# Low parts of 24 weight tiles formed by accumulating transfers, with a new order of block one

## The chip, the core and the metric

The kernel runs on one core of one Trainium2 chip. The metric is the device time of one execution in microseconds. The core has a matrix engine (PE in the profile, with its weight loads as PEld), a vector engine (DVE), a scalar engine (ACT), GpSimd (POOL) and SyncE (SP). SP starts nearly all transfers between the chip's memory (HBM) and the on-chip memory (SBUF). PE writes its results into eight PSUM banks, from where DVE or ACT take them out.

## The reference

Two layers run one after the other on 512 positions of width 1024, batch 1, all in float32. Block one projects the normalised input with one wide matrix and feeds two branches from it: a recurrence over time (eight heads of 64), and an attention that keeps, for each query, the 128 keys with the highest index scores.

```python
xn = rmsnorm(x, norm_g)
p = xn @ w_in                                     # 24 tiles of 128 columns here
p_shift, g_rwkv, q_down, kv_down, k_idx_raw, w_idx, g_attn = jnp.split(p, IN_SPLITS, axis=-1)
...
S = S * w_t + sa * (kk_t * a_t) + v_t * k_t       # rwkv7_scan, over time
y_rwkv = y * jax.nn.silu(gate)
...
_, idx = lax.top_k(score, topk)                   # topk = 128
p = jax.nn.softmax(s, axis=-1)                    # over the chosen keys
y_attn = o * jax.nn.silu(gate)
x = x + jnp.concatenate([y_rwkv, y_attn], axis=-1) @ w_out
```

Block two mixes three branches (a gated 3-tap convolution, a 31-tap convolution with a layer norm, an attention on 256 memory rows), adds a feed-forward net with 2816 channels, and normalises. Its memory rows give keys with `w_k` and values with `w_v`, before anything of block one is known.

## The kernel before

All activations lie transposed: 128 channels on the partitions, 512 positions along a row. A float32 product is made of three fast products (type fp32r). Each operand is split into a high part H, which is its value rounded to fp32r, and a low part L = value − H. PE adds up H·H, H·L and L·H and leaves L·L out. For a weight tile of 128 output columns and 1024 rows (`slab`, L547) SP brings the raw tile into one of four `wr` buffers, ACT writes H into one of three `wh` buffers, and DVE writes L = raw − H into one of three `wl` buffers (`sub`, L353). A tile of `w_in` then takes 24 matmuls with 512 columns: eight rows of blocks, each with two matmuls on H and one on L. `out_half` (L1302) does the same for half a tile of `w_out` (four rows of blocks, 12 matmuls); half 0 takes the recurrence's channels, half 1 those of the attention. The tiles of `w_v` have two rows of blocks with 512 columns, and H and L are the moving operand there (also 12 matmuls). `w_k` is multiplied in plain float32, raw.

`w_in` numbers 0 to 15 are the latents, keys, receptances and values; 16 to 23 are the two gates (`strand_gates`, "gr" and "ga"), which are first needed when a branch ends. The memory strand (`w_k`, `w_v`) is needed in block two alone.

The program is written as a list of operations with groups ("level"), and `Program.order` (L188 on) puts them into one order: it goes on in its own estimate of time, takes of all operations that could start the one that starts first, and among those nearly equal the one with the lowest rank. A rank is the operation's number plus 20000 times its group's entry in the table `LEVEL`. The order is fixed at build time. Each engine executes its own share strictly in that order and waits at semaphores. So a wait of one instruction holds everything behind it on its engine.

In block one the serial work is this: projections, the inverses of 32x32 triangles on DVE, the chain over eight chunks (`strand_chain`), beside it the top-k for three query blocks (16 times MAX8 and MATCH_REPLACE8 on DVE each, `strand_index`), the heads, the attention (`strand_attention`), and last `w_out`. Tiles of weights that nothing waits for yet fill PE in between. GpSimd sets constants, masks the scores, and multiplies the chain's state (`G.tensor_mul`, two for each chunk).

Nearly every operation carries the line of the recorder (L341), `sub` L354, and those that may go to either engine L345 to L360; so tiles name them: `wr`, `wh`, `wl` are weights, `a` activations, `s` small columns, `ps` PSUM, `x` the inverses.

Of the kernel before, what the change touches and what calls it, by code (L numbers as in the profile page):

```python
# [8 lines left out]
F32 = mybir.dt.float32  # L9
F32R = mybir.dt.float32r  # L10
AF = mybir.ActivationFunctionType
ALU = mybir.AluOpType
# [13 lines left out]
NA = 76  # L26
NS = 12
LEVEL = {
# [12 lines left out]
}  # L41
MEMC = 4
BOOST = 0
# [43 lines left out]
class Program:  # L87
# [73 lines left out]
    def cost(self, who, op, outs, ins):  # L161
        n = outs[0].free_size()
        if op == "dma_start":
            return 0.06
        if who == "PE":
            if ins[0].dtype != F32:
                return max(0.0535, n / 2400.0) + 0.0132
            if op == "transpose":
                return 0.107
            m = outs[0].shape[0]  # L170
            return 2 * max(0.107 if m > 64 else 0.056 if m > 32 else 0.029, 2 * n / 2400.0)
        n = max(x.free_size() for x in outs + ins)
        narrow = sum(x.free_size() == 1 for x in ins[1:])
        if who == "V":
            if op in ("max", "match_replace", "tensor_tensor_reduce"):
                return 0.07 + 0.06 * (op == "match_replace") + n / 960.0
            if op in ("tensor_tensor_scan", "transpose"):
                return 0.07 + n / 490.0
            if op == "tensor_mul" and ins[1:] and ins[1].ap[-1][0] > 1 and ins[1].ap[-1][1] > 1:
                return 0.07 + n / 500.0  # L180
            fast = op in ("tensor_copy", "tensor_scalar") and all(x.space != PSUM for x in ins + outs)
            scalar = op == "scalar_tensor_tensor" and len(ins) > 2
            return 0.069 + 0.064 * (scalar or narrow > 0 and op == "tensor_scalar") + n / (1920.0 if fast else 960.0)
        if who == "S":
            return (0.058 if ins[0].space == PSUM else 0.085) + 0.092 * (narrow + len(outs) - 1) + n / 1175.0
        return 0.07 + n / (1250.0 if op == "memset" else 440.0)
# [132 lines left out]
def build(tc, I, O, plan=None):  # L319
# [33 lines left out]
    def sub(out, x, y):  # L353
        prog.add({"V": ("tensor_sub", lambda: nc.vector.tensor_sub(out, x, y))}, [out], [x, y])  # L354
# [34 lines left out]
    def here():  # L389
        return len(prog.nodes) - 1  # L390

    V, S, G, PE, SY = (Queue(e, w) for e, w in ((nc.vector, "V"), (nc.scalar, "S"), (nc.gpsimd, "G"),
                                                 (nc.tensor, "PE"), (nc.sync, "SY")))

    def pooled(pool, shape, dt, tag):
        k = len(pools)
        if plan is None:
            t = pool.tile(list(shape), dt, tag=tag, name=tag, bufs=caps[tag])
        else:
            t = pool.tile(list(shape), dt, tag="%s%d" % (tag, plan[2][k]), name=tag, bufs=1)  # L400
        pools.append(t.tensor.name)
        prog.tag[t.tensor.name] = tag
        return t
# [10 lines left out]
    def A(shape=(128, 512), dt=F32):  # L414
        return pooled(ap_, shape, dt, "a")
# [4 lines left out]
    def SM(n, m=128):  # L420
        return pooled(sp, (m, n), F32, "s")

    def PS():
        return pooled(pp, (128, 512), F32, "ps")
# [106 lines left out]
    def rsqrt(src, n, eps, op=ALU.add, scale=1.0):  # L531

        x, y, t = SM(n), SM(n), SM(n)
        ts(V, x, src, scale, eps, ALU.mult, op)
        ts(V, t.bitcast(I32), x.bitcast(I32), 1, None, ALU.logical_shift_right)
        ts(V, y.bitcast(I32), t.bitcast(I32), -1.0, float(0x5F3759DF), ALU.mult, ALU.add)
        for _ in range(3):
            V.tensor_mul(t, y, y)
            V.scalar_tensor_tensor(t, t, -0.5, x, op0=ALU.mult, op1=ALU.mult)
            V.scalar_tensor_tensor(y, t, 1.5, y, op0=ALU.add, op1=ALU.mult)  # L540
        return y


    def WR(shape):
        return pooled(wp, [128] + list(shape), F32, "wr")

    def slab(name, idx, shape=(8, 128), parts=1):  # L547
        nk = min(shape[0], 8 if name != "w_down" or idx % 3 < 2 else 6)
        raw = WR(shape)
        SY.dma_start(raw[:, 0:nk, :], I[name][idx][:, 0:nk, :])  # L550
        H = pooled(wp, (128,) + shape, F32R, "wh")
        L = pooled(wp, (128,) + shape, F32R, "wl")
        for p in range(parts):
            k = slice(nk * p // parts, nk * (p + 1) // parts)
            S.activation(H[:, k, :], raw[:, k, :], AF.Copy)
            sub(L[:, k, :], raw[:, k, :], H[:, k, :].bitcast(F32))
        return H, L, nk

    def gemm_tile(name, idx, xH, xL, n=512, ps=None, k0=0, ktot=8, parts=1):
        H, L, nk = slab(name, idx, parts=parts)  # L560
        ps = ps or PS()
        for k in range(nk):
            kk = k0 + k
            PE.matmul(ps[:, :n], H[:, k, :], xH[kk], start=kk == 0, stop=False)
            PE.matmul(ps[:, :n], H[:, k, :], xL[kk], start=False, stop=False)
            PE.matmul(ps[:, :n], L[:, k, :], xH[kk], start=False, stop=kk == ktot - 1)
        return ps
# [111 lines left out]
    raw = A()  # L679
    wix = AR_()  # L680
    raw, wix = raw[:, 0:64].rearrange("p (k c) -> p k c", k=8), wix[:, 0:64].rearrange("p (k c) -> p k c", k=8)
# [620 lines left out]
    def out_half(n, half):  # L1302
        raw = WR((4, 128))
        SY.dma_start(raw, I["w_out"][n][:, 4 * half:4 * half + 4, :])
        H = pooled(wp, (128, 4, 128), F32R, "wh")
        L = pooled(wp, (128, 4, 128), F32R, "wl")
        S.activation(H, raw, AF.Copy)
        sub(L, raw, H.bitcast(F32))
        ps = PS()
        for k in range(4):  # L1310
            h, l = yH[4 * half + k], yL[4 * half + k]
            PE.matmul(ps, H[:, k, :], h, start=k == 0, stop=False)
            PE.matmul(ps, H[:, k, :], l, start=False, stop=False)
            PE.matmul(ps, L[:, k, :], h, start=False, stop=k == 3)
        return ps

    for n in range(8):
        xr = A()
        with after(here()):
            SY.dma_start(xr, I["xt"][n])  # L1320
        with level("out%d" % n):
            V.tensor_add(xr, out_half(n, 0), xr)
        X1.append(xr)
    prog.group, prog.offset = "rest", int(LEVEL["rest"] * 20000)
    for n in range(8):
        xr = X1[n]
        V.tensor_add(xr, out_half(n, 1), xr)
        h, l = split_act(xr, Dp("gz", n))
        zH.append(h)
        zL.append(l)  # L1330
        sq = A()
        S.activation(sq, xr, AF.Square)
        ac2 = add_to(ac2, sq, Dp("fgs", n))
        ac1 = add_to(ac1, sq)
# [3 lines left out]
    r1 = rsqrt(sv[:, 0:4], 4, 1e-6)  # L1338
    r2 = SM(4)
    V.tensor_mul(r2, r1, r1)  # L1340
    V.tensor_mul(r2, r2, sv[:, 4:8])
    r2 = rsqrt(r2, 4, 1e-6)
# [81 lines left out]
    for s_ in range(4):  # L1424
        GV = []
        for m in range(2):
            n = 2 * s_ + m
# [99 lines left out]
    for f in range(22):  # L1527
        gu = []
        for m in range(2):
            n = f + 22 * m  # L1530
# [16 lines left out]
    for n in range(7):  # L1547
# [7 lines left out]
        scaled(X3[n], X3[n], P_("fin_g", n))  # L1555

    last = [slab("w_down", 21 + j) for j in range(3)]
    for half in range(2):
        hs = slice(256 * half, 256 * half + 256)
        ps = PS()  # L1560
        for k in range(22):
            H, L = (t[:, k % 8, :] for t in last[k // 8][:2])
# [19 lines left out]
        r2 = rsqrt(st[:, 0:2], 2, 1e-6)  # L1582
# [115 lines left out]
```

## Time and profile before

| | us |
|---|---|
| runs: median (lowest, highest) of 3 | 1377.17 (1376.52, 1382.12) |
| the profiled execution's own time | 1377.95 |
| its span in the trace | 1376.2 |
| PE busy | 1348.1 (98%) |
| DVE busy | 1049.8 (76%) |
| ACT busy | 585.4 (43%) |
| POOL busy | 29.9 (2%) |

The profiled execution took 1377.95 us, 1.75 us more than its span; it stands 0.8 us above the median of the runs. An engine's busy time is the union of its instructions' durations. PE's matmuls are pipelined and their ends are modelled, so a busy PE still can have gaps. Block one ends at about 399.6 us of the span, and from there to 1340 us PE is busy without a gap that the windows show.

### The profile page before, as it was taken

The page shows a single profiled execution, that of the slowest core. Times are in us where ns is not written, and L with a number is a line of the kernel's source. Part 1 is how long each engine was busy: PE and PEld are TensorE (multiplying, and loading weights), DVE is VectorE, ACT ScalarE, POOL GpSimd, SP SyncE. Part 2 cuts the span into 40 slices and gives each one's busy share as a digit, 9 for nine tenths or more (in the row PEclk, how much of TensorE's full clock was granted, in tenths as well). Part 3 has the DMA queues.
Part 4 walks back from the last instruction along what each step waited for, and adds up shares of the span by engine and source line. Part 5 has one row for each costly group of instructions (what it writes and reads, how often), then busy time and mean ns, then how long its engine had stood idle before and what let it go on. Part 6 is the DMA issues. An engine that isn't in the chain of part 4 may idle for free.

```text
span 1376.2 us, 18233 instructions
## 1 busy us (share of the span) xinstructions
PE 1348.1 (98%) x7032; PEld 1121.8 (82%) x7032; DVE 1049.8 (76%) x1902; ACT 585.4 (43%) x945; POOL 29.9 (2%) x68
## 2 busy tenths in 40 slices
PE   7999999999999999999999999999999999999997
PEld 6878877888888888888888878888888888888886
DVE  7699879999699999999993584444577788784333
ACT  6683455668353334322222372223444444442221
POOL 2010002100000000000000000000000000000000
PEclk9999988999999999999999999999999999999999
DMA  6203220031446221233333223233222333322321
GB/s 225 71 20 104 84 72 32 32 100 55 145 146 214 92 77 62 77 101 99 92 98 101 77 92 107 92 98 101 92 92 95 104 92 96 103 88 96 100 70 61
DMA packets 41927, 129.29 MB, mean 94 GB/s; under 512 B 4912, under 2 KB 7088, under 8 KB 41840
## 3 DMA queue, kind: packets, MB, share of 16 engines
q1 hardware_dynamic: 41840, 128.13, 28.8%
q8 instruction: 55, 0.90, 0.3%
q14 instruction: 32, 0.26, 0.1%
HBM read 123.91 MB, written 4.19 MB: 93 GB/s over the span
## 4 chain that ended last, share of the span: by engine, by line
PE 88%; DVE 7%; ACT 3%; issue 1%; POOL 0%; DMA 0%; DVEq 0%; POOLq 0%; ACTq 0%
PE ps L341 88%; DVE a L341 5%; ACT a L341 2%; DVE s L341 1%; DVE wl L354 0%; DVE a L354 0%; ACT a L346 0%; ACT wh L341 0%; DMA wr<-in_w_v 0%; POOL a L341 0%; DVE a L345 0%; POOL mm L341 0%; DVE x L345 0%; ACT a L350 0%; POOL gsel L341 0%
## 5 line engine op out<-in xcount | busy, mean ns | idle before, releaser
L341 PE MATMUL ps<-a,wh 128*128 128x512 f32 (+1 forms) x3276 | 1006.2, 388 | 0.2 <-ACT wh L341 0.2
L341 PEld LDWEIGHTS ps<-a,wh 128*128 128x128 f32 x3276 | 612.1, 188 | 123.5 <-ACT wh L341 0.8
L341 PE MATMUL ps<-a,wl 128*128 128x512 f32 (+1 forms) x1638 | 634.7, 388 | 0.5 <-DVE wl L354 0.5
L341 ACT ACTIVATE wh<-wr 128x1024 fp32r<-128x1024 f32 (+3 forms) x223 | 224.8, 1010 | 490.6 <-PE ps L341 362.3
L341 PEld LDWEIGHTS ps<-a,wl 128*128 128x128 f32 x1638 | 308.2, 188 | 62.8 <-DVE wl L354 1.0
L354 DVE TENSOR_TENSOR wl<-wr,wh 128x1024 fp32r<-128x1024 f32 (+3 forms) x223 | 257.9, 1159 | 78.2 <-ACT wh L341 76.8
L341 DVE SCALAR_TENSOR_TENSOR a<-a,par 128x511 f32<-128x511 f32 (+24 forms) x393 | 273.4, 730 | 5.5 <-ACT a L341 3.1
L341 DVE TENSOR_TENSOR a<-ps,a 128x512 f32<-128x512 f32 (+1 forms) x186 | 117.2, 632 | 113.2 <-PE ps L341 107.2
L341 ACT ACTIVATE a<-a 128x512 f32<-128x512 f32 (+5 forms) x184 | 112.3, 623 | 169.5 <-DVE a L341 151.2
L341 PE MATMUL ps<-a 128*64 128x64 f32 (+10 forms) x1060 | 134.3, 296 | 14.5 <-POOL a L341 7.5
L341 PEld LDWEIGHTS ps<-a 128*64 128x64 f32 (+5 forms) x1040 | 103.5, 170 | 27.3 <-DVE a L341 5.7
L341 DVE SCALAR_TENSOR_TENSOR a<-a 128x512 f32<-128x512 f32 (+3 forms) x112 | 67.7, 611 | 20.3 <-ACT a L341 19.4
L341 DVE TENSOR_TENSOR a<-a 128x512 f32<-128x512 f32 (+5 forms) x134 | 76.0, 585 | 3.0 <-ACT a L341 1.9
L341 ACT ACTIVATE a<-a,par 128x512 f32<-128x512 f32 (+1 forms) x89 | 65.1, 737 | 19.7 <-DVE a L341 18.0
L354 DVE TENSOR_TENSOR a<-a 128x512 fp32r<-128x512 f32 x72 | 48.4, 686 | 18.1 <-ACT a L341 16.1
L341 ACT ACTIVATE a<-ps 128x512 fp32r<-128x512 f32 (+5 forms) x77 | 42.1, 569 | 44.4 <-PE ps L341 33.5
L341 DVE SCALAR_TENSOR_TENSOR a<-a,ps 128x512 f32<-128x512 f32 x24 | 16.5, 686 | 55.5 <-PE ps L341 55.4
L341 ACT ACTIVATE a<-a,dpar 128x512 f32<-128x512 f32 (+2 forms) x57 | 41.6, 733 | 7.6 <-DVE a L341 7.3
L346 ACT ACTIVATE a<-ps 64x256 f32<-64x256 f32 (+5 forms) x74 | 29.5, 409 | 28.3 <-PE ps L341 26.9
L341 PE MATMUL ps<-ident,a 128*128 128x128 f32 x204 | 32.7, 286 | 1.0 <-ACT a L350 0.6
L341 PEld LDWEIGHTS ps<-ident,a 128*128 128x128 f32 x204 | 25.8, 155 | 7.2 <-ACT a L350 1.7
L341 PE MATMUL ps<-a,wr 128*128 128x256 f32 x128 | 29.6, 379 | 0.0
(113 smaller groups left out, 567.7 us busy)
## 6 DMA issues: line engine op xcount, KB each, us to landing
wr<-in_w_in SPq DMA_DIRECT2D x96, 512.0 KB, 3.6
wr<-in_w_up SPq DMA_DIRECT2D x44, 512.0 KB, 3.4
wr<-in_w_down SPq DMA_DIRECT2D x16, 512.0 KB, 3.5
a<-in_xt SPq DMA_DIRECT2D x16, 256.0 KB, 3.5
wr<-in_w_k SPq DMA_DIRECT2D x8, 512.0 KB, 3.6
wr<-in_w_v SPq DMA_DIRECT2D x8, 512.0 KB, 3.6
wr<-in_w_out SPq DMA_DIRECT2D x16, 256.0 KB, 2.7
wr<-in_w_att SPq DMA_DIRECT2D x8, 512.0 KB, 3.5
```

The lines of the kernel that those rows point to most:

```text
L341: prog.add({self.who: (op, lambda: f(*a, **k))}, outs, ins)
L346: "S": ("activation", lambda: nc.scalar.activation(out, src, AF.Copy))}, [out], [src])
L354: prog.add({"V": ("tensor_sub", lambda: nc.vector.tensor_sub(out, x, y))}, [out], [x, y])
```

## The change

The low part can be made in another way. A new function `low` has ACT write −H (rounded like H) into the `wl` buffer, by an activation with scale −1, and has GpSimd start a transfer from HBM that adds the raw weights to what stands there (`accum_op=ALU.add`). DVE's subtraction falls away for the tiles that go this way: `w_in` 16 to 23, all eight tiles of `w_v`, and the 16 half tiles of `w_out`, which makes 32 transfers of 24 tiles' bytes. The table `LEVEL` is replaced as a whole, and the order's own estimate of a transfer's issue on GpSimd goes from 0.06 to 1.0 us. `slab` and `out_half` call `low`; nothing else is changed.

```diff
 LEVEL = {
-    "att0": -0.214, "att1": 1.055, "att2": -0.113, "att3": 1.636, "base": 2.048, "chain": -0.643, "first":
...
+    "att0": 0.372, "att1": -0.274, "att2": 2.672, "att3": 2.806, "base": 0.757, "chain": 2.012, "first":
...
         if op == "dma_start":
-            return 0.06
+            return 1.0 if who == "G" else 0.06
...
+    def low(L, raw, H, src, dma):
+
+        if dma:
+            S.activation(L, raw, AF.Copy, scale=-1.0)
+            G.dma_start(L, src, accum_op=ALU.add)
+        else:
+            sub(L, raw, H.bitcast(F32))
+
...
             S.activation(H[:, k, :], raw[:, k, :], AF.Copy)
-            sub(L[:, k, :], raw[:, k, :], H[:, k, :].bitcast(F32))
+            low(L[:, k, :], raw[:, k, :], H[:, k, :], I[name][idx][:, k, :], name == "w_v" or name == "w_in" and idx > 15)
...
         S.activation(H, raw, AF.Copy)
-        sub(L, raw, H.bitcast(F32))
+        low(L, raw, H, I["w_out"][n][:, 4 * half:4 * half + 4, :], True)
```

What this does to the order is shown at three places. The first is ACT at the second halves of `w_out`, the last work of block one. `wh<-wr` makes H, `a<-a,dpar` and `a<-a` belong to the sum that has come out. Before:

```order
248 L341 ACTIVATE wh<-wr 128x512
249 L341 ACTIVATE a<-a,dpar 128x512
250 L341 ACTIVATE a<-a 128x512
251 L341 ACTIVATE wh<-wr 128x512
252 L341 ACTIVATE a<-a,dpar 128x512
```

Now, with `wl<-wr`, which writes −H:

```order
289 L341 ACTIVATE wh<-wr 128x512
290 L341 ACTIVATE wl<-wr 128x512
291 L341 ACTIVATE a<-a,dpar 128x512
292 L341 ACTIVATE a<-a 128x512
293 L341 ACTIVATE wh<-wr 128x512
294 L341 ACTIVATE wl<-wr 128x512
```

Each half tile now takes two of ACT's instructions in a row, and its low part is ready only when the transfer behind the second has landed.

The second place is GpSimd's queue from the inverse to the start of the chain (`AFFINE_SELECT wr<-wr` and `MEMSET x_403` prepare the inverse, `AFFINE_SELECT a<-a` masks scores, `TENSOR_TENSOR a<-a,pc` is the chain's state). Before:

```order
33 L341 AFFINE_SELECT wr<-wr 128x1024
34 L341 MEMSET a 64x512 x2
35 L341 MEMSET x_403 32x32x32 x2
36 L341 AFFINE_SELECT a<-a 128x128 x2
37 L341 TENSOR_TENSOR a<-a,pc 128x256 x2
```

Now:

```order
32 L341 AFFINE_SELECT wr<-wr 128x1024
33 L341 DMA wl<-in_w_in 128x1024
34 L341 MEMSET a 64x512 x2
35 L341 DMA wl<-in_w_in 128x1024 x3
36 L341 MEMSET x_403 32x32x32 x2
37 L341 DMA wl<-in_w_in 128x1024 x4
38 L341 AFFINE_SELECT a<-a 128x128 x2
39 L341 TENSOR_TENSOR a<-a,pc 128x256 x2
```

The eight transfers for the gates stand ahead of the masks of the top-k and of the chain. Those of `w_v` and `w_out` (24 in all) stand behind the chain's last product, as the last work of this queue in block one.

The third place is PE at the end of the attention (`ps<-a 64x128` are the last products of the attention, `ps<-a,wh` and `ps<-a,wl` are `w_out`, `ps<-a,wr` is `w_k`, `ps<-wh,a` is `w_v`). Before:

```order
657 L341 MATMUL ps<-a,wr 128x256 x5
658 L341 MATMUL ps<-ident,a 128x128 x4
659 L341 MATMUL ps<-a,wr 128x256 x4
660 L341 MATMUL ps<-a 64x128 x32
661 L341 MATMUL ps<-a,wh 128x512 x2
662 L341 MATMUL ps<-a,wl 128x512
```

Now:

```order
666 L341 MATMUL ps<-a,wh 128x512 x2
667 L341 MATMUL ps<-a,wl 128x512
668 L341 MATMUL ps<-a,wr 128x256 x7
669 L341 MATMUL ps<-a 64x128 x37
670 L341 MATMUL ps<-wh,a 128x512
671 L341 MATMUL ps<-wl,a 128x512
672 L341 MATMUL ps<-wh,a 128x512 x2
```

Before, all `w_out` stands behind the last products of the attention, and all `w_v` ahead of them. Now six half tiles of `w_out` stand ahead of them, and four tiles of `w_v` behind.

## Rows read from the trace of the kernel before

**Rows 1.** The page: busy us, share of the span, instructions

```profile
PE 1348.1 (98%) x7032; PEld 1121.8 (82%) x7032; DVE 1049.8 (76%) x1902; ACT 585.4 (43%) x945; POOL 29.9 (2%) x68
```

**Rows 2.** Windows: length, busy (instructions) by engine, granted clock, DMA share, GB/s

```profile
0.00:25.00 25.00, 17.47 (x82) 13.86 (x83) 19.07 (x39) 16.62 (x26) 8.18 (x36) 1.00 0.78 262
...
103.00:190.00 87.00, 85.88 (x531) 71.92 (x530) 72.24 (x144) 35.79 (x51) 3.46 (x5) 0.96 0.29 94
190.00:275.00 85.00, 78.52 (x839) 66.48 (x838) 80.06 (x243) 53.17 (x125) 11.55 (x21) 0.92 0.11 36
275.00:352.40 77.40, 76.60 (x502) 64.90 (x501) 76.84 (x260) 55.87 (x135) 0.00 (x0) 1.00 0.25 79
352.40:399.60 47.20, 47.20 (x211) 39.21 (x210) 34.55 (x58) 20.60 (x35) 0.00 (x0) 1.00 0.47 151
...
408.00:725.00 317.00, 317.00 (x1468) 264.29 (x1468) 314.60 (x504) 103.18 (x147) 0.00 (x0) 1.00 0.32 103
```

**Rows 3.** The same windows, DVE's writes of `wl` alone

```profile
103.00:190.00 87.00, 15.84 (x13) 0.96 0.29 94
190.00:275.00 85.00, 1.21 (x1) 0.92 0.11 36
275.00:352.40 77.40, 7.46 (x7) 1.00 0.25 79
352.40:399.60 47.20, 10.82 (x15) 1.00 0.47 151
```

**Rows 4.** The chain of waits from 190 to 352.4 us, by line

```profile
by line: PE ps L341 47.9%; DVE a L341 22.1%; DVE s L341 8.9%; ACT a L341 4.5%; DVE a L354 4.0%; issue 3.5%; DMA wr<-in_w_v 2.2%; DVE wl L354 1.8%; DVE a L345 1.1%; ACT a L346 1.1%; ACT wh L341 1.0%; DVE x L345 0.9%; ACT a L350 0.7%; DVE a L
```

**Rows 5.** Timeline of DVE: first MAX8, last product of the attention

```profile
198.50 0.55 DVE L341 MAX8 s<-a 128x8 f32<-128x384 f32 x1
...
353.74 0.88 DVE L341 SCALAR_TENSOR_TENSOR a<-ps,a 128x128 f32<-128x128 f32 x4
```

**Rows 6.** Groups by form, 0 to 620 us: busy us, mean ns, idle before

```profile
L354 DVE TENSOR_TENSOR wl<-wr,wh 128x1024 fp32r<-128x1024 f32 x68 | 82.7, 1218 | 2.1 <-ACT wh L341 1.8
L341 ACT ACTIVATE wh<-wr 128x1024 fp32r<-128x1024 f32 x68 | 71.9, 1059 | 142.3 <-PE ps L341 115.6 <-issue 18.5 <-DMA wr<-in_w_v 5.5
...
L354 DVE TENSOR_TENSOR wl<-wr,wh 128x512 fp32r<-128x512 f32 x16 | 11.0, 686 | 7.8 <-ACT wh L341 7.8
...
L341 ACT ACTIVATE wh<-wr 128x512 fp32r<-128x512 f32 x16 | 10.1, 629 | 18.0 <-PE ps L341 15.6 <-issue 1.7 <-ACT a L341 0.7
```

**Rows 7.** Timeline of ACT in `w_out`, half 0: idle before, releaser

```profile
363.43 0.63 ACT L341 ACTIVATE wh<-wr 128x512 fp32r<-128x512 f32 x1 [2.09 <-PE ps L341]
366.15 0.63 ACT L341 ACTIVATE wh<-wr 128x512 fp32r<-128x512 f32 x1 [2.09 <-PE ps L341]
```

**Rows 8.** Tile `wl`, 0 to 400 us: duration min/median/max, first and last start

```profile
L341 PE MATMUL ps<-a,wl x256: 387/389/628, 9.5 to 399.3; 128*128 128x512 f32 x128
```

**Rows 9.** Transfers issued from 0 to 420 us: KB each, median us to landing

```profile
wr<-in_w_v SPq DMA_DIRECT2D x8, 512.0 KB, 3.6
wr<-in_w_out SPq DMA_DIRECT2D x16, 256.0 KB, 2.7
...
a<-in_wsm SPq DMA_DIRECT2D x6, 256.0 KB, 4.9
...
par<-in_pars SPq DMA_DIRECT2D x1, 246.0 KB, 7.8
```

**Rows 10.** Timeline of POOL: a mask over 128x1024

```profile
100.60 2.93 POOL L341 TENSOR_SCALAR_AFFINE_SELECT wr<-wr 128x1024 f32<-128x1024 f32 x1
```

22 rows, old and new, of the table LEVEL are left out of this document.

## Prediction

> **What bounds the kernel now.** I read the page's first part, then windows over block one, then the chain of waits and the timelines inside the slowest stage. The page says PE 98% [rows 1]: no engine but PE can bound the whole, and the only time to be had is where PE has gaps. After 399.6 us PE is busy without any, with DVE at 314.6 of 317 beside it [rows 2]; there the change does nothing. So all is decided before 399.6 us, where `w_out`'s last low part starts at 399.3 [rows 8].
>
> Block one has three stages. Up to 190 us PE leads: 85.88 of 87 us busy against DVE's 72.24 [rows 2]. From the first MAX8 at 198.5 to the attention's last product on DVE at 353.74 + 0.88 = 354.6 us [rows 5] DVE leads: from 190 to 352.4 us it is busy 80.06 + 76.84 = 156.9 of 162.4 us, 96.6%, while only 47.9% of the chain of waits lies on PE [rows 2, 4]. In the last stage, 352.4 to 399.6, PE is full (47.20 of 47.20) and DVE is not (34.55) [rows 2]. A microsecond taken off DVE counts in the middle stage, and hardly elsewhere.
>
> **What is removed.** DVE loses 8 subtractions for the gates and 8 for `w_v` at 1.218 us, and 16 for `w_out` at 0.686: 9.7 + 9.7 + 11.0 = 30.4 us [rows 6]. Where they stood: 13 in the PE-led stage (15.84 us, the gates' among them), 8 in the DVE-led stage (1.21 + 7.46 = 8.67 us), 15 in the full-PE stage (10.82 us) [rows 3]. So 8.67 us stood where DVE sets the pace: worth 8.67 x 0.966 = 8.4 us at most. The rest hid behind PE and is worth nothing to 399.6 us.
>
> **What is added on ACT.** 16 writes of −H at 1.06 and 16 at 0.63 us, 27 us [rows 6]. ACT is busy 109.0 of 162.4 us in the middle stage and 20.60 of 47.20 in the last [rows 2]; four tiles of `w_v` (4.2 us) and some six half tiles of `w_out` (3.8 us) fall into the middle stage and bring it to 117 of 162. I cost the busy time at 0; where ACT's softmax pieces queue behind a pair of weights, at most one pair (2.1 us) is late, and that end I keep for the range.
>
> **What moves.** Counting PE's order, 623 matmuls with 512 columns stood ahead of the first MAX8 and 622 do now, so the top-k starts about where it did. Between it and the attention's last product there were 187 and there are 208; behind it 184, now 164. One such matmul takes 2.72/12 = 0.227 us, since ACT's `wh` follows at 2.72 us from half tile to half tile of 12 [rows 7]. The last stage is shorter by 20 x 0.227 = 4.5 us, and the middle one takes 21 x 0.227 = 4.8 us more of PE. If these all fall into PE's gaps the move gains 4.5; if they stand in the way of the serial chain it gains 0. The order shows both: six half tiles of `w_out`, 72 matmuls or 16 us, and two products of `w_k` now stand ahead of PE's last 37 matmuls of the attention, at a point where DVE has its softmax pieces behind it. There PE leads again, and a DVE that is done sooner waits for PE. So a good part of the 8.4 us is spent on a PE that has got its filler later than DVE wanted it. Of 8.4 + 4.5 = 12.9 us I take a third, 4 us; the ends are 0 and 12.9.
>
> **The new wait.** A low part was there 1.2 us after H. Now it needs −H and then a transfer that reads HBM and adds into SBUF; PE's third matmul of each tile waits for it, and behind it all of PE. No such transfer is in the trace. Lower end: SyncE's plain transfers of the same bytes, 2.7 us for 256 KB and 3.6 for 512 [rows 9]. Upper end: 7.8 us, the latest landing of about 256 KB among these rows, and 8.7 for 512 KB by the same 0.9 us more [rows 9]. Nearer by content is `wsm`, 256 KB at 4.9 us [rows 9].
>
> What each costs follows from how far ahead ACT runs. In the last eight half tiles, three `wl` buffers go round in 3 x 2.72 = 8.16 us; in that time come H and −H (0.63 each), some 0.3 for three hand-overs (an estimate from rows 7: H starts at a regular 2.72 us), the landing, and 10 of 12 matmuls before the buffer is free (2.27). So a landing of up to 8.16 − 1.26 − 0.3 − 2.27 = 4.3 us costs nothing, and each microsecond above it a third of one per half tile. At the tight places before them I counted PE's matmuls between what releases ACT's −H and the first use of L: the third tile of the late `w_v` has 14 (3.2 us) for 1.06 + 0.3 + landing; the last two gates 6.6 and 7.4 us for 2.12 + 0.3 + landing; the fourth half tile of `w_out` 4.75 us for 1.26 + 0.3 + landing.
> - At 2.7 / 3.6 us: only the `w_v` tile is late, 1.06 + 0.3 + 3.6 − 3.2 = 1.8: 2 us.
> - At 4.9 / 5.8 us: eight half tiles x 0.2 = 1.6; `w_v` 4.0; gates 1.6 + 0.8; early `w_out` 1.7: 10 us.
> - At 7.8 / 8.7 us: 8 x 1.2 = 9.3; `w_v` 7; gates 4.5 + 3.7; early `w_out` 4.6 and two behind it about 2: 31 us.
>
> I take the middle of the two lower pairs, 3.8 / 4.7, because the transfers are no longer than SyncE's but GpSimd must issue them: last tiles 0, `w_v` 2.9, gates 0.5, early `w_out` 0.6: 4 us.
>
> The Trainium skill ("DMA: Bandwidth & Descriptors", Measured and Specifications) gives 0.95 us for 64 KB and 6.15 for 1 MB for plain transfers that GpSimd issues, without the issue, and a first byte after about 1 us. By it, as an estimate, 256 KB land after 3.0 and 512 KB after 4.4 us, and the stalls would be 3 us instead of 4; an accumulating transfer has no price there, and no transfer of GpSimd is in this trace to compare with.
>
> **GpSimd's queue.** The eight gate transfers each wait for their −H, with the clearing of the inverses' tile behind four of them and the top-k's masks and the chain's first state product behind all eight. The longest instruction this queue showed took 2.93 us [rows 10]; a transfer that keeps it as long would still be through ahead of the masks, since the last gate's first low matmul comes earlier in PE's order than the top-k. I cost it at 0. The 24 others have nothing of block one behind them.
>
> **The transfers' share.** The additional 24 tiles are 12.6 MB read. In the last stage the engines were at 0.47 with 151 GB/s, and the start showed 262 GB/s at 0.78 [rows 2]. Half tiles twice (raw and low) are 0.52 MB in 2.72 us, 193 GB/s: room is left, unless an addition counts double (289).
>
> **Sum.** −4 (DVE and order) + 0 (ACT) + 4 (late low parts) = 0: 1377.95 + 0 = 1378 us, 0.8 us above the median of the runs. Differences under 0.5%, 6.9 us, can't be told from none.
>
> **Rivals.**
> - Relief counts in full, landings like SyncE's: −12.9 + 2 = −11, 1367 us. For it: DVE at 96.6%, the shorter last stage. Against it: PE's filler ahead of the attention's last matmuls. 0.29.
> - The low parts land late and PE stands at every tile in the last stages. It decides from a landing of about 6 us on for 256 KB: there the same places give 17 − 4 = +13; at the upper end +31 − 4 = +27, 1405 us. Its middle is 1390. For it: three buffers leave 4.3 us, and rows 9 show landings of 4.9 and 7.8 for such sizes. Against it: most of SyncE's land in 2.7 to 3.6. 0.23.
> - The accumulation is quick but DVE is the wrong engine to relieve: the order gives PE's gaps back in the middle stage. No gain, 4.8 us of PE in the chain's way, 4 of stalls: +9, 1387 us. For it: 52% of the chain of waits in that stage is off PE, in many short steps [rows 4]. Against it: PE has gaps there. 0.08.
> - The transfers wait for DVE. DVE has next to no pauses from 190 to 352.4 us [rows 2], and if GpSimd could write a transfer's commands only between two of its instructions, a landing grows by up to 0.69 us, the length of one; then 4.5 / 5.4 us, stalls of 7, 1381 us, within no change. The skill ("SBUF — State Buffer", Who interferes with whom, and the warning on the "DVE blocks DMA" trap) speaks against the change here: a transfer issued from GpSimd took about 3.1 us instead of 0.62 beside a DVE copy, so 2.5 us more. By that each landing would be 5.2 / 6.1 us, the stalls 12, and the time 1386. The trace of before has no such transfer to show it. It names copies and tensor-scalar operations, few here; so I leave this in the chances of the others.
>
> **Chances.** No change 0.40 (1371 to 1384), faster 0.29 (1363 to 1371), slower 0.31 (the second and third rival). The range that holds 8 in 10 leaves the best tenth below 1364 and the worst tenth above 1396, between the second rival's middle and its end.
>
> **What would show it.** Right: landings of 3.5 to 5 us for the new transfers, PE's `wl` matmuls waiting 1 to 4 us at a few tiles, the first MAX8 within 3 us of 198.5, DVE under 90% from there to the attention's end, block one ending at 396 to 404 us. Wrong: PE pausing at the third matmul of every half tile, at a period over 2.72 us (late low parts); or block one ending before 392 us (the relief counts).

## The result, and the profile after

The changed kernel takes 1431.05 us (median of 4 runs, 1429.89 to 1433.51), the kernel before 1377.42 beside it: a ratio of 1.037 on record, with a 95% interval from 1.0346 to 1.0395 (the two medians alone give 1.039). It is slower by 54 us, far outside the range of 1364 to 1396. The profiled execution took 1430.86 us, 1429.2 of them its span.

Part 1 of the page of the changed kernel answers to [rows 1]:

```profile
PE 1368.1 (96%) x7032; PEld 1130.6 (79%) x7032; DVE 1029.1 (72%) x1880; ACT 604.7 (42%) x967; POOL 55.1 (4%) x100
```

PE has the same 7032 matmuls, and takes 20 us more for them. The span grew by 53 us: the other 33 are PE standing still. DVE lost 20.7 us, not 30.4: by the counts ten instructions that either engine may run went from ACT to it (1902 − 32 + 10 = 1880, and 945 + 32 − 10 = 967).

Windows of the changed kernel, columns as in [rows 2]:

```profile
103.00:190.00 87.00, 81.64 (x379) 66.71 (x378) 59.75 (x131) 37.76 (x52) 12.72 (x14) 0.94 0.49 113
190.00:275.00 85.00, 74.75 (x825) 62.78 (x824) 76.16 (x223) 48.28 (x109) 9.86 (x19) 0.92 0.16 47
275.00:352.40 77.40, 66.45 (x466) 54.36 (x465) 62.51 (x227) 47.51 (x117) 6.53 (x9) 0.91 0.37 89
352.40:399.60 47.20, 42.17 (x250) 34.17 (x251) 22.68 (x70) 25.66 (x48) 6.02 (x7) 0.97 0.60 151
399.60:460.00 60.40, 51.29 (x214) 40.50 (x213) 31.80 (x47) 29.28 (x45) 9.50 (x11) 0.94 0.71 174
460.00:725.00 265.00, 265.00 (x1238) 221.32 (x1238) 262.85 (x432) 88.98 (x131) 0.00 (x0) 1.00 0.31 103
```

Behind 460 us PE is full, as it was behind 399.6 before: all is lost in block one. Its last low part starts at 452.3 us (tile `wl` of the changed kernel, to be read as [rows 8]), 53.0 later than before:

```profile
L341 PE MATMUL ps<-a,wl x256: 387/389/793, 9.2 to 452.3; 128*128 128x512 f32 x128
```

What PE waited for from 100 to 470 us in the changed kernel (in all, times, longest):

```profile
PE ps L341 <- DMA wl<-in_w_v: 16.3, 4, 5.9
PE ps L341 <- DMA wl<-in_w_out: 6.2, 6, 1.7
PE ps L341 <- DMA wl<-in_w_in: 5.2, 2, 3.9
```

That is 27.7 us at low parts that had not landed. The transfers of the changed kernel, in the view of [rows 9], and its queues (packets, MB, share of 16 engines over the span):

```profile
wl<-in_w_in POOLq DMA_DIRECT2D x8, 512.0 KB, 7.5
wr<-in_w_v SPq DMA_DIRECT2D x8, 512.0 KB, 5.0
wl<-in_w_v POOLq DMA_DIRECT2D x8, 512.0 KB, 8.7
wr<-in_w_out SPq DMA_DIRECT2D x16, 256.0 KB, 3.6
wl<-in_w_out POOLq DMA_DIRECT2D x16, 256.0 KB, 5.2
...
q1 hardware_dynamic: 41840, 128.13, 28.2%
q0 software_dynamic: 4608, 12.58, 5.0%
```

The low parts landed after 5.2 us (256 KB) and 7.5 to 8.7 (512 KB); the forecast was 3.8 and 4.7. SyncE's own loads of the same weights became later too: 3.6 to 5.0 and 2.7 to 3.6 [rows 9]. The queues say why the additions are heavy. GpSimd's 12.58 MB held the engines for 5.0% of 1429.2 us, or 71.5 us, which is 176 GB/s, against 318 for SyncE (128.13 MB in 403 us): 1.8 times the time per byte.

The chain of waits of the changed kernel at the first two tiles of `w_v` whose low part came late (start, length, what), and PE's timeline behind the first:

```profile
292.91 10.34 DMA wl<-in_w_v
...
316.60 6.60 DMA wl<-in_w_v
```

```profile
303.29 0.80 PE L341 MATMUL ps<-wl,a 128*128 128x512 f32 x1 [5.89 <-DMA wl<-in_w_v]
...
304.74 0.63 PE L341 MATMUL ps<-wl,a 128*128 128x512 f32 x1
...
314.57 0.40 PE L341 MATMUL ps<-wl,a 128*128 128x512 f32 x1
```

PE stood 5.89 us, and then ran its 512 columns in 0.63 us a piece where it later takes 0.40. Three windows of the changed kernel, the first the pause, the others behind two waits:

```profile
297.40:303.30 5.90, 0.01 (x2) 0.01 (x1) 4.45 (x16) 3.30 (x8) 1.69 (x2) 0.85 1.03 288
303.30:310.40 7.10, 7.08 (x34) 5.87 (x34) 0.96 (x4) 0.38 (x1) 0.00 (x0) 0.64 0.67 152
...
411.70:417.00 5.30, 5.30 (x13) 4.14 (x14) 0.00 (x0) 1.10 (x2) 0.18 (x1) 0.50 0.92 237
```

In the pause the DMA engines were full (1.03); behind it the granted clock was 0.64, and behind the wait that ended at 411.65 it was 0.50, the lower of the two levels. So a wait of 5 us costs PE some 2 to 3 us more (7.1 x 0.36 and 5.3 x 0.50 are 2.6 each). Over the five windows to 460 us, length times missing clock is 24.0 us against 10.3 in [rows 2]: up to 13.7 us more.

### The profile page after: what moved, and what is told of

Its sections match the earlier page's. It is cut to its first block, busy times and chain, and to the rows that moved or that the text cites. A ratio compares the mean times of both kernels' runs of the same rounds, so it can differ in the third digit from the quotient of the medians.

```text
span 1429.2 us, 18317 instructions
## 1 busy us (share of the span) xinstructions
PE 1368.1 (96%) x7032; PEld 1130.6 (79%) x7032; DVE 1029.1 (72%) x1880; ACT 604.7 (42%) x967; POOL 55.1 (4%) x100
## 3 DMA queue, kind: packets, MB, share of 16 engines
q1 hardware_dynamic: 41840, 128.13, 28.2%
q0 software_dynamic: 4608, 12.58, 5.0%
## 4 chain that ended last, share of the span: by engine, by line
PE 78%; DVE 7%; issue 5%; DMA 5%; ACT 4%; POOL 1%; SPq 0%; DVEq 0%; POOLq 0%; ACTq 0%
PE ps L341 78%; DVE a L341 4%; ACT a L341 3%; DMA wl<-in_w_out 2%; DMA wl<-in_w_v 2%; DVE s L341 1%; DMA wl<-in_w_in 1%; POOL wl L341 0%; DMA a<-in_xt 0%; ACT a L360 0%; ACT wh L341 0%; DVE a L354 0%; DVE a L345 0%; DVE wl L354 0%; ACT a L346 0%
## 5 line engine op out<-in xcount | busy, mean ns | idle before, releaser
L354 DVE TENSOR_TENSOR wl<-wr,wh 128x1024 fp32r<-128x1024 f32 (+1 forms) x191 | 227.8, 1196 | 71.4 <-ACT wh L341 69.7
L341 DVE SCALAR_TENSOR_TENSOR a<-a,par 128x510 f32<-128x510 f32 (+23 forms) x393 | 273.0, 733 | 5.3 <-ACT a L341 3.1
L341 DVE TENSOR_TENSOR a<-ps,a 128x512 f32<-128x512 f32 (+2 forms) x186 | 117.5, 634 | 145.6 <-PE ps L341 130.1
L341 PE MATMUL ps<-a 128*64 128x64 f32 (+9 forms) x1060 | 134.8, 294 | 16.1 <-POOL a L341 7.3
L341 ACT ACTIVATE a<-ps 128x512 f32<-128x512 f32 (+5 forms) x77 | 42.2, 571 | 47.5 <-PE ps L341 37.4
L346 ACT ACTIVATE a<-ps 64x256 f32<-64x256 f32 (+5 forms) x66 | 24.8, 398 | 41.4 <-PE ps L341 39.4
L345 DVE COPY a<-ps 128x256 f32<-128x256 f32 (+5 forms) x31 | 15.7, 511 | 35.6 <-PE ps L341 35.3
```

The lines of the kernel that those rows point to most:

```text
L341: prog.add({self.who: (op, lambda: f(*a, **k))}, outs, ins)
L345: prog.add({"V": ("tensor_copy", lambda: nc.vector.tensor_copy(out, src)), "S": ("activation", lambda: nc.scalar.activation(out, src, AF.C ...
L346: "S": ("activation", lambda: nc.scalar.activation(out, src, AF.Copy))}, [out], [src])
```

## The experiments

Theory 1: the low parts land late, and PE waits for them. Theory 2: the newly searched order is itself worse. "Block one" is the start of its last matmul on `wl`, in the row shown above for the changed kernel (399.3 us before); the ratio is to the kernel before, run on the same chip. The runs come from several chips, on which the kernel before took 1377 to 1383 us, so rows are better compared by ratio than by median. Block one is read from the profiled execution; that of the old order without transfers took 1385.88 us, 5 above its median.

| run | median us | ratio (95% interval) | block one |
|---|---|---|---|
| changed kernel | 1431.05 | 1.037 (1.0346 to 1.0395) | 452.3 |
| its order, no transfer | 1386.87 | 1.0061 (1.0044 to 1.0079) | 408.7 |
| its order, DVE adds | 1410.64 | 1.0228 (1.021 to 1.0245) | 427.5 |
| its order, `w_v` alone | 1411.63 | 1.0217 (1.0186 to 1.0249) | 434.5 |
| its order, `w_out` alone | 1395.62 | 1.0105 (1.0075 to 1.0135) | 416.4 |
| its order, gates alone | 1397.2 | 1.0117 (1.0083 to 1.015) | 417.8 |
| its order, plain transfers | 1399.47 | 1.013 (1.0099 to 1.0162) | 422.5 |
| its order, in halves | 1417.33 | 1.0253 (1.0224 to 1.0282) | 438.4 |
| old order, transfers | 1436.72 | 1.0418 (1.04 to 1.0436) | 458.4 |
| old order, no transfer | 1380.59 | 1.0008 (0.9991 to 1.0025) | 406.6 |
| old order, DVE adds | 1393.21 | 1.0082 (1.0052 to 1.0112) | 414.1 |
| old priorities, planned without transfers | 1379.36 | 1.0003 (0.999 to 1.0016) | 401.4 |
| planner told, new priorities | 1414.69 | 1.0258 (1.0228 to 1.0288) | 436.4 |
| planner told, old priorities | 1429.53 | 1.0368 (1.0336 to 1.04) | 456.6 |

**The order with no transfer.** Every engine's order as in the changed kernel.

```diff
             S.activation(L, raw, AF.Copy, scale=-1.0)
-            G.dma_start(L, src, accum_op=ALU.add)
+            prog.add({"G": ("dma_start", lambda: None)}, [L], [src])
```

> The changed kernel's order on every engine with the 32 transfers left out, so that the low parts of the 24 tiles hold -H alone (the addition of the weights is what is left out). It shows what relief of DVE and order are worth together when a low part comes early. Theory 1: 1362 to 1378 us, 5 to 10 below the run with the addition on DVE, PE's wait on wl under 3 us in all. Theory 2: 1410 us or more, as the order's gaps stay.

It took 1386.87 us. Theory 1's range is missed by 9 us and theory 2's by 23, but 44 of the 54 us are gone with the transfers: theory 1 has the bulk. The order by itself is slower by 0.6%, some 8 us, although DVE has 32 subtractions less. Its windows (190 to 275 us, and the stage from its first MAX8 to the attention's last product), and then that stage in the kernel before and in the changed one:

```profile
190.00:275.00 85.00, 75.04 (x861) 63.68 (x861) 79.01 (x241) 50.58 (x117) 11.25 (x21) 0.88 0.12 36
...
193.90:366.60 172.70, 161.68 (x1462) 136.67 (x1461) 148.13 (x497) 114.14 (x260) 10.96 (x20) 0.94 0.23 70
```

```profile
198.50:354.60 156.10, 148.82 (x1309) 126.85 (x1308) 151.80 (x497) 102.60 (x246) 11.16 (x20) 0.96 0.18 59
```

```profile
204.10:393.70 189.60, 165.88 (x1462) 137.83 (x1461) 148.53 (x496) 113.97 (x260) 22.12 (x33) 0.93 0.33 85
```

Without transfers the stage starts 4.6 us sooner and takes 16.6 longer, 12.9 of these in PE's busy time (153 matmuls more, and a lower clock); behind it 2.6 are won back. Of the 153, 21 have the 512 columns that the prediction counted (4.8 us), and 128 are the small 32x32 products of the inverses (2.4 us of PE), which stood ahead of the first MAX8 before, from 176.4 us on. PE rather than DVE now holds this stage: DVE is at 148.13 of 172.70, and from 180 to 370 us its longest waits are for PE (in all, times, longest; in the kernel before all its waits for PE in this stage came to 1.7 us):

```profile
DVE a L345 <- PE ps L341: 15.2, 2, 12.1
```

With the transfers the stage takes 189.6.

**The old order, with the transfers and without.** PE's order as in the kernel before; −H and the transfer stand where the subtraction stood. The second run leaves the transfer out.

```diff
+            nc.scalar.activation(L, raw, AF.Copy, scale=-1.0)
+            nc.gpsimd.dma_start(L, src, accum_op=ALU.add)
...
-            sub(L[:, k, :], raw[:, k, :], H[:, k, :].bitcast(F32))
...
-        sub(L, raw, H.bitcast(F32))
```

> The order of the kernel before on PE, with -H on ACT and the accumulating transfer on GpSimd put where DVE's subtraction stood, for the same 24 tiles. Theory 1: as late as in the changed kernel, since three buffers give each low part the same few us: 1405 to 1450 us, with PE's waits on wl of 20 us or more. Theory 2 (the order): within 10 us of the kernel before, 1367 to 1387.

> The order of the kernel before, -H on ACT in place of DVE's subtraction for the 24 tiles, and no transfer (the addition of the weights is what is left out). It prices the relief alone in the old order. If the 8.7 us of subtractions in the stage that DVE leads count in full, 1367 to 1371 us; if PE and the serial chain take them back, 1375 to 1379. Both theories allow either; it bounds what any transfer could have won there.

With the transfers 1436.72, without 1380.59. So the transfers cost 56 us in the old order and 44 in the new: theory 2 falls as the main cause. Some 9 to 10 of the 56 fall at a place that the new order does not have: a gate's tile is the first of all here, and PE's first product on a low part starts at 18.6 us, where it is 9.5 before [rows 8] and 8.3 in the old order without transfers.

```profile
L341 PE MATMUL ps<-a,wl x256: 387/389/796, 18.6 to 458.4; 128*128 128x512 f32 x128
```

And taking 30 us off DVE, with ACT's 27 us of −H in their place, is worth nothing in the old order: the ratio's interval holds 1. The stage from the first MAX8 to the attention's last product, without transfers:

```profile
202.66:361.34 158.68, 150.66 (x1308) 127.89 (x1307) 144.18 (x488) 109.73 (x255) 11.13 (x20) 0.95 0.18 58
```

DVE is busy 7.6 us less than before, yet the stage is not shorter: DVE now waits 7.1 us for PE in it and 5.4 for ACT, before 1.7 and 0.9. What the relief would be worth without ACT's writes was not tried.

**The old priorities, planned for a DVE that is free.** The `G.dma_start` is gone, so the planner knows that a low part costs only ACT's write; priorities of the kernel before.

> No transfer at all (the addition of the weights is left out for the 24 tiles, low parts hold -H), the priorities of the kernel before, and a planner that knows that DVE is free of these subtractions. It tells whether 30 us less on DVE are worth something once the order is made for it. If DVE sets the middle stage: 1366 to 1371 us. If PE and the serial chain set it: 1374 to 1382.

1379.36 us, a ratio of 1.0003, in the second range. An order that knows of the relief gains nothing from it either. Within that interval (0.999 to 1.0016), no transfer, however quick, could have won time with these priorities and −H on ACT.

**One class of tiles at a time.** The changed kernel's order; one class keeps its transfers.

```diff
-            G.dma_start(L, src, accum_op=ALU.add)
+            if src.tensor.name == "in_w_v":      # or "in_w_out", or "in_w_in"
+                G.dma_start(L, src, accum_op=ALU.add)
+            else:
+                prog.add({"G": ("dma_start", lambda: None)}, [L], [src])
```

> The changed kernel's order with the accumulating transfer kept for the 8 tiles of w_v alone; the low parts of gates and w_out hold -H (their addition is left out). Against the 1386.9 us without any transfer. Theory 1 (late landings at single places, added up): PE's 16.3 us of waiting on w_v's low parts, and up to 8 us of half clock behind them: 1403 to 1412 us. Rival (the 24 transfers crowd each other and SyncE's loads, and each alone is harmless): under 1394 us, landing of w_v's at 5 us or less.

> The same with the transfers of the 16 half tiles of w_out alone (w_v and gates hold -H). Theory 1: 6.2 us of waits and up to 6 of clock and loads: 1392 to 1400 us, landing near 5 us. Rival (crowding): within 3 us of 1387, landing under 4.3 us, the limit of the three buffers.

> The same with the transfers of the 8 gate tiles of w_in alone (w_v and w_out hold -H). Theory 1: 5.2 us of waits and one or two spells of half clock, 1391 to 1398 us. Rival (crowding): within 3 us of 1387. Over the three runs the gains over 1387 add up to 35 to 50 us by theory 1, to under 15 by the rival.

PE's waits of the three runs, one fence each:

```profile
PE ps L341 <- DMA wl<-in_w_v: 15.5, 4, 5.1
```

```profile
PE ps L341 <- DMA wl<-in_w_out: 7.3, 5, 2.3
```

```profile
PE ps L341 <- DMA wl<-in_w_in: 5.3, 3, 4.2
```

All three times are in theory 1's ranges. Against 408.7 us without transfers, block one ends 25.8, 7.7 and 9.1 us later: 42.6 of the 43.6 that the changed kernel shows. By the ratios the three add up to 2.6% of the 3.1%. The costs add, so the crowding of one class by another is not to blame. Four waits at `w_v` are more than half. Each is longer than the pause alone: 15.5 us of waiting cost 25.8, with the clock behind it.

**Plain transfers in place of additions.** The same issues, without `accum_op`.

```diff
-            G.dma_start(L, src, accum_op=ALU.add)
+            G.dma_start(L, src)
```

> The changed kernel with GpSimd's 32 transfers as plain copies without the addition (the low part becomes the weights themselves; the subtraction is what is left out). Theory 1a (the addition makes the transfer slow: it moved 176 GB/s while busy, SyncE's 318): landings fall to 3 to 3.6 us for 256 KB and 4 to 4.7 for 512, share of the engines per byte like SyncE's, 1392 to 1408 us. Theory 1b (GpSimd's way of issuing is what takes long): landings within 0.7 us of 5.2 and 7.5 to 8.7, and 1420 us or more.

Its transfers and GpSimd's queue:

```profile
wl<-in_w_in POOLq DMA_DIRECT2D x8, 512.0 KB, 4.7
...
wl<-in_w_v POOLq DMA_DIRECT2D x8, 512.0 KB, 5.2
...
wl<-in_w_out POOLq DMA_DIRECT2D x16, 256.0 KB, 4.1
...
q0 software_dynamic: 4608, 12.58, 2.8%
```

1399.47 us: 32 of the 44 us go with the addition. Landings are 4.1, 4.7 and 5.2, at or a little above what theory 1a said, and the engines are held 39 us for the same bytes: 321 GB/s, like SyncE's. What remains over no transfer, 10 us by the ratios and 13 by the medians, is what GpSimd's plain transfers and their share cost in these places.

**Landing alone.** A program that does nothing else, one transfer after the other.

```diff
+                nc.scalar.activation(t, raw[:, 0:n, :], AF.Copy, scale=-1.0)
...
+                    eng.dma_start(t, src(k, n), accum_op=ALU.add)   # or without; SyncE or GpSimd
```

> No part of the computation (the output is zeros): one transfer after the other, each behind ACT's write of the same tile, of 256 and 512 KB: SyncE plain, GpSimd plain, GpSimd with addition, and GpSimd with addition beside a DVE that copies without pause. Theory 1a (the addition itself is slow): with addition 4.6 to 5.2 and 6.7 to 7.7 us, plain by GpSimd 2.9 to 4 and 3.8 to 4.7, SyncE 2.7 and 3.6. Rival (the crowd of other transfers made them slow): with addition within 0.7 us of GpSimd's plain. Beside DVE's copies: the same within 0.3 us if DVE doesn't hold GpSimd's writing of a transfer's commands, 1 us or more longer if it does.

Its transfers ("a" 256 KB, "b" 512; "beside" is with a DVE that copies without pause), and GpSimd's time for an issue (min/median/max):

```profile
sync_b<-in_w_in SPq DMA_DIRECT2D x5, 512.0 KB, 3.3
plain_b<-in_w_in POOLq DMA_DIRECT2D x5, 512.0 KB, 3.6
add_b<-in_w_in POOLq DMA_DIRECT2D x5, 512.0 KB, 5.4
beside_b<-in_w_in POOLq DMA_DIRECT2D x5, 512.0 KB, 5.4
...
sync_a<-in_w_in SPq DMA_DIRECT2D x5, 256.0 KB, 2.6
plain_a<-in_w_in POOLq DMA_DIRECT2D x5, 256.0 KB, 2.9
add_a<-in_w_in POOLq DMA_DIRECT2D x5, 256.0 KB, 3.9
beside_a<-in_w_in POOLq DMA_DIRECT2D x5, 256.0 KB, 4.1
```

```profile
L335 POOL DMA_DIRECT2D add_a<-in_w_in x5: 851/861/889, 42.1 to 61.3; - x5
```

```profile
L335 POOL DMA_DIRECT2D beside_a<-in_w_in x5: 860/1255/1322, 152.1 to 171.9; - x5
```

The addition by itself adds 1.0 us to 256 KB and 1.8 to 512, less than theory 1a said and more than its rival's 0.7. So the landing in the kernel has two parts: 3.9 and 5.4 us alone, and another 1.3 and 2.1 to 3.3 beside other transfers. In the run with `w_v`'s transfers alone they landed after 8.8 us, so additions of the other classes are not the reason. In the packet records the first data of an addition starts 1.6 us after the issue here, and 1.6 to 5.1 us in the changed kernel. Two causes can be seen there, though no run takes them apart. The addition issued at 292.91 us shares the engines with loads that SyncE issued at 292.64 and 293.99: its data goes from 295.5 to 301.5 us. The additions issued at 297.37 and 300.64 begin their data at 301.5 and 304.5, each when the one before it in GpSimd's queue is through.

**In halves.** Each transfer becomes two, the second right behind the first.

```diff
-            G.dma_start(L, src, accum_op=ALU.add)
...
+                nc.gpsimd.dma_start(L[:, :h, :], src[:, :h, :], accum_op=ALU.add)
+                nc.gpsimd.dma_start(L[:, h:, :], src[:, h:, :], accum_op=ALU.add)
...
```

> The changed kernel with each of the 32 transfers issued as two halves one behind the other (256 + 256 KB, 128 + 128 KB), so that the first matmuls on a low part need only the first half. If the landing of the first piece is what PE waits for (theory 1): a lone 256 KB took 3.9 us against 5.4, so w_v's and the gates' ten or so stalls are 1.5 to 2.5 us shorter each and w_out's 0.5 to 1, and the time falls by 10 to 25 us, to 1406 to 1421. If the bytes that the additions move set the pace, or GpSimd's second issue (0.86 us) delays as much as the half gains: 1426 to 1440.

PE's waits in this run:

```profile
PE ps L341 <- DMA wl<-in_w_v: 11.9, 5, 3.8
PE ps L341 <- DMA wl<-in_w_out: 5.8, 6, 1.8
...
PE ps L341 <- DMA wl<-in_w_in: 3.4, 2, 2.5
```

1417.33 us, 14 less (16 by the ratios) with the same bytes, order and places, as expected if the first piece is what PE waits for. `w_v` and the gates gain 6.2 us of waits, `w_out` 0.4: halving helps the large tiles.

**DVE adds in the transfers' place, in both orders.** −H stays on ACT.

```diff
-            G.dma_start(L, src, accum_op=ALU.add)
...
+                nc.vector.tensor_add(L, raw, L.bitcast(F32))
...
```

> The changed kernel's order on every engine, the write of -H on ACT kept, but the 32 transfers replaced by an addition on DVE (L = raw + L, 24 tiles in 32 pieces) right behind the write of -H. Theory 1 (the transfers land late, and PE waits for the low parts at the tight places): the 52 us are the transfers' alone, so block one ends again near 400 us and the time is 1370 to 1390 us. Theory 2 (the newly searched order is itself worse, its gaps in the middle stage would be there with any low part): 1415 us or more, with block one ending behind 435 us.

> The order of the kernel before, with -H on ACT and then an addition on DVE for the 24 tiles, no transfer: the form of the earlier run with the addition on DVE, in the old order. If that form is what cost 24 us there (DVE stands until ACT has written -H, 15.9 us in the DVE-led stage): 1392 to 1408 us. If the new order cost it, having no room for these 30 us on DVE: 1377 to 1386, like DVE's plain subtraction in this order.

1410.64 and 1393.21: the first lies between both theories, the second at the lower end of its first range (1392 to 1408), which says that the form itself costs time. DVE's waits from 190 to 400 us, in the new order and in the old:

```profile
DVE wl L552 <- ACT wl L551: 15.9, 12, 3.7
```

```profile
DVE wl L550 <- ACT wl L549: 15.2, 14, 2.3
```

In this form DVE stands behind ACT's −H for 15 us in either order, and over no transfer that costs 13 us in the old order (10 by the ratios) and 24 in the new. So the run in the new order does not undo the transfers alone: it brings a wait of its own. About half of its 24 us is the form. The rest fits an order that has no room left for 30 us on DVE, which was not shown further.

**A planner that knows the landing.** The planner's due times for GpSimd's transfers:

```diff
-                dma = max(dma, t + 1.2) + n["bytes"] / 360e3
-                end = dma + 0.8
+                slow = e == "G"
+                dma = max(dma, t + 1.2) + n["bytes"] / (176e3 if slow else 360e3)
+                end = max(dma + 0.8, t + 2.3 + n["bytes"] / 90e3 if slow else 0.0)
```

> The changed kernel whole, but its planner is told what the transfers took in the changed kernel's trace (landing 2.3 us + bytes at 90 KB/us after the issue: 5.2 us for 256 KB, 8.1 for 512; the engines held at 176 KB/us) in place of SyncE's figures; the priorities are the new ones, so the planner puts other work where PE stood. Theory 1 (PE waits because the order sets the first use too close behind the issue): PE's wait on wl falls from 27.7 us to under 8 and the time to 1385 to 1405 us. Rival (three buffers and the transfers' share set the pace, whatever the order): 1418 us or more.

> The same with the priorities of the kernel before. Theory 1: 1380 to 1400 us, PE's wait on wl under 8 us. Rival: 1418 us or more. By neither is it faster than the kernel before, since the old order without any transfer took 1380.6.

PE's waits, first with the new priorities (the longest three and `w_out`), then with the old:

```profile
PE ps L342 <- ACT a L347: 5.7, 2, 5.3
PE ps L342 <- DMA wl<-in_w_v: 4.8, 3, 2.2
PE ps L342 <- DVE a L355: 4.7, 2, 4.2
...
PE ps L342 <- DMA wl<-in_w_out: 2.8, 3, 1.5
```

```profile
PE ps L342 <- DVE s L342: 25.4, 5, 21.1
```

With the new priorities the waits at low parts fall from 27.7 to 7.6 us, as theory 1 said, but the time only to 1414.69: the chain of ACT and DVE is now what PE stands for. With the old ones PE stands 21.1 us for the top-k, and the time is 1429.53. A gate's transfer again goes out at the very start, at 6.9 us, and PE's first product on a low part starts only at 20.2. The first time lies between both expectations; the second is in the rival's range, but hardly for the rival's reason, as PE waits 4.7 us for low parts in the whole run. Each set of priorities was searched for other due times, so these two runs do not tell what a search with the right ones would reach. No version here beats the kernel before.

## Why the prediction was wrong

- **What bounds the kernel: right in the large.** All was decided in block one, and PE is full behind it. But DVE's 96.6% in the middle stage was read as a pace that relief could speed up. In the same rows PE is at 78.52 + 76.60 = 155.1 of 162.4 us, 95.5%, so they did not single out DVE. Two runs without transfers, at 1.0008 and 1.0003, show that relief with −H on ACT is worth nothing there: in the first of them DVE spent what it had gained waiting for PE and ACT.
- **The failed step: the landing of an addition.** It was taken as 3.8 / 4.7 us, the middle between SyncE's plain transfers and `wsm`. That is what GpSimd's plain transfers take here (4.1 and 4.7 to 5.2). With the addition it was 5.2 and 7.5 to 8.7: for 512 KB the upper end of the bounds, for 256 KB the middle level. The term was 4 us; the waits were 27.7, near its own upper end of 31, but in part at other places.
- **The places: those named were late, three others too.** With the measured landings the prediction's own sums give 6.9 us for the third late tile of `w_v`, 5.8 for the gates and 4.4 for `w_out`; 4.86, 5.2 and 6.2 came. The tiles left out were the first of `w_v` at 303 us, the fourth at 323 and the second late one at 397: 5.89 + 3.50 + 2.06 = 11.45 us. The first one's addition was issued 5.8 us after its raw load, between two of SyncE's next loads. The fourth's raw load was issued 22.6 us ahead of its addition, which went out only when PE released it at 316.6 us, 3.1 us before PE came to need the tile.
- **The clock: not in the sum at all.** Behind each long wait PE ran at a granted 0.50 to 0.64 for 5 to 7 us: up to 13.7 us.
- **The order: wrong sign.** Relief and order together were put at −4 (ends −12.9 and 0); alone they are +7.6 by the medians, +9.4 at block one's end. That is the third rival's mechanism; it had 0.08. That 1386.87 is nearly its 1387 us is chance, since its sum holds 4 us of stalls that this run does not have. The count of 21 more matmuls of 512 columns in the middle stage was right, but all matmul records there grew by 153.
- **The sum as it was.** 9.4 (order) + 27.7 (waits) + up to 13.8 (clock, 24.0 against 10.2 in the run without transfers, whose four other windows are at 1.00) = 50.9 of 53.0 us. PE's busy time agrees on the clock: 1368.1 us against 1353.2 in that run, 14.9 more for the same matmuls. The second rival (late low parts, 0.23) named the mechanism, and priced it too low: 1405 at its upper end.
- **ACT and GpSimd's queue at 0: little speaks against it.** PE's longest wait for a weights write by ACT was 1.0 us, and GpSimd's first mask for the top-k waited for PE, not for a transfer. DVE's 5.4 us of waits for ACT in the old order without transfers are the one sign of a price on ACT.
- **The transfers' share.** "Room is left, unless an addition counts double": it counts 1.8 times, by the queues of two runs, 5.0% against 2.8% for the same bytes.
- **Transfers that wait for DVE: a small thing.** Beside DVE's copies the issue of 256 KB took 1.26 us instead of 0.86, and the landing 4.1 instead of 3.9 (512 KB: 0.91 and 5.4, the landing as alone). The Trainium skill ("SBUF — State Buffer", Who interferes with whom) names this direction, and the issue agrees. The roughly 2.5 us more that the Trainium skill gives on the same page (A bandwidth-pool intuition that's wrong) are not seen here.
- **The signs named.** Landings of 3.5 to 5, the first MAX8 within 3 us (204.1, so 5.6 late) and block one's end at 396 to 404 all failed; DVE fell under 90% (148.53 of 189.6, 78%). PE did not pause at every half tile: 6 of 16 in `w_out`, 6.2 us.

## What to carry to other kernels

A busy share near 97% does not make an engine the bound: leave its work out in one run, and see whether the time falls, before paying for relief. When a step on the chip is replaced by a transfer, price its landing beside the loads that are queued with it, then look for each first use that stands closer behind the issue than that. Add what PE loses in clock behind a wait of several us.

## What the runs showed of the hardware

- An accumulating transfer from HBM into SBUF held the DMA engines 1.8 times as long per byte as a plain one (5.0% against 2.8% of the span for 12.58 MB), and GpSimd was busy 0.86 us for its issue, 0.53 for a plain one.
- Alone it landed after 3.9 us (256 KB) and 5.4 (512 KB), plain by GpSimd after 2.9 and 3.6, by SyncE after 2.6 and 3.3. For GpSimd's plain ones the estimate worked out from the Trainium skill ("DMA: Bandwidth & Descriptors", Measured and Specifications) was 3.0 and 4.4: the first agrees, the second is long.
- Loads beside it were slower: SyncE's eight loads of `w_v` landed after 5.0 us (median) beside all the additions, 4.1 beside `w_v`'s alone, 4.3 beside plain transfers and 3.8 beside none.
